# A two-layer hybrid decoder trunk on one core: moving operands of TensorE read in two interleaved runs, whole tiles as one product of 512 columns

## The chip, the core and the metric

The kernel runs on one core of one Trainium2 chip. Its time is device time in microseconds (us), median of several runs. The core has TensorE (PE in the profile, its weight loads PEld), VectorE (DVE), ScalarE (ACT), GpSimd (POOL) and SyncE (SP), an on-chip memory of 128 partitions (SBUF) and an accumulation memory (PSUM) into which TensorE writes.

## The reference

A trunk of two layers over 512 tokens of width 1,024. Layer 0 mixes tokens by attention in three groups of 8 heads (windows 128, 512 and 2,048 at dilations 1, 4 and 16, joined by a softmax over the groups), layer 1 by a gated linear recurrence with a causal convolution of four taps. Each is followed by a gated feed-forward part (FFN) with a causal convolution of three taps. Each part stands between two RMS norms and is added to the residual stream. Cut to what matters:

```python
for layer in range(DEPTH):
    h = rms_norm(x, norm_mix_pre[layer])
    h = dilated_attention_mixer(h, ...) if layer % 2 == 0 else rglru_mixer(h, ...)
    x = x + rms_norm(h, norm_mix_post[layer])
    h = rms_norm(x, norm_ffn_pre[layer])
    h = conv_ffn(h, ...)      # (gelu(conv(h @ w_up)[:D_FF]) * conv(h @ w_up)[D_FF:]) @ w_down
    x = x + rms_norm(h, norm_ffn_post[layer])

def causal_dwconv(x, w, b):   # along the tokens
    out = b
    for k in range(K):
        out = out + xp[:, k:k + S] * w[k]
    return out
```

## The kernel before

**Split products.** All large products are made in three passes: each f32 operand is split into a high part in TensorE's faster f32 format (fp32r) and a low part, the rest (`split`, L211: the high part by ACT at L212, the low part by DVE at L213), and hi*hi, hi*lo and lo*hi are added up in PSUM (`mm3`, L476, its products at L478). The profile writes f32 for these operands too. The scores S, the attention outputs O of the strided heads and the transposes tr are plain f32 products.

In `mm(dst, l, r)` the second argument is the stationary operand, loaded as weights (128 columns a load), and the third is the moving operand, whose columns stream through the array. The profile names the moving one first: `ps<-hT,whi` has hT moving, `acc<-whi,ahi` has the weight moving.

**Who moves.** There are two kinds.
- Tokens move. The normed tokens lie transposed in hT (features on the partitions, 512 tokens in a row, a high and a low copy), and a tile of 128 output features is a sum over 8 blocks of features. `feat` (L687) makes one half of a tile, 256 tokens; `feat_tile` (L720) makes both halves one after the other; `feat_tiles` can also make the first halves of several tiles before the second halves, at the start of the FFNs and of the recurrent layer, where the later tokens are not ready yet; `quarters` (L1138) makes one tile in four steps between others. The strided q and k of attention and FFN columns of blocks 2 to 11 are made by `chain` (L1157) in a scheme of seven block products instead of eight, 84 products of 256 columns for two tiles, on blocks of hT and on sums of them (T, last). `rights` (L1126) picks the moving block of each step.
- Weights move. Values (`first_values` L1293, `products` L1362) have tokens stationary and 512 columns of weights moving. The output projections of attention and recurrence (`rows_proj`, L731, `product` at L756) and the FFN's second product (`down`, L947, and `rows`, L1208) have activations stationary, 128 tokens a tile, and 512 weight columns moving, and end in acc. In the gates of the recurrent layer (L1680) tokens move, 512 columns.

**Order.** The kernel is emitted by hand in the order in which each engine runs it. Weights come in by DMA from SP (`load`, L403) and are split ahead of use by `pump` (L367), called at each `tick`; the sums of weight blocks for the chains are made by DMAs that add and by DVE. Steps of the chains stand in tables (`AT`, `QUAD`).

**Around the products.** q and k of the local heads are scaled by DVE into natural token order (`qk`, L1281); those of the strided heads are put in order of token mod 4 in the same instruction (`permute`). The convolutions read PSUM shifted by one to three columns, so the tokens must stand there in a row. The residual stream X has four tiles of 128 tokens, rows of tokens in a row; it is read from x at the start, again after attention (`x_again`, L1008), and written to out by `postnorm` (L664). The host lays out the weights before the run (`_laid_out`, L107).

Of the kernel before, what the change touches and what calls it, by code (L numbers as in the profile page):

```python
# [18 lines left out]
P = 128  # L19
S = 512  # L20
D = 1024
# [82 lines left out]
    return w.reshape(n, P, 2048)  # L104


def _laid_out(name, value):  # L107

    a = np.asarray(value)
    if name == "attn_w_qkv":  # L110
        cols, out = _column_blocks(a[0], True), []
        for kind, at, *cuts in _qkv_order():
            if kind == "value":
                rows = a[0][at * 512 : at * 512 + 512].reshape(P, 4, -1)
                out.append(np.concatenate([rows[:, :, c0 : c0 + m] for c0, m in cuts[0]], 2).reshape(P, 2048))
            else:
                out.append(cols[at // 256])
        return np.stack(out)
    if name == "lru_w_in":
        return _column_blocks(a[0], False)  # L120
    if name == "ffn_w_up":
        return np.stack([_column_blocks(w, False) for w in a])
    return a


@with_exitstack
def kernel(
# [536 lines left out]
    def postnorm(t, banks, g, final):  # L664
        at = [slice(0, 512), slice(512, 1024)]
        parts = banks
        u = [gen(s="post") for _ in at]

        def gained(i):
            nc.vector.tensor_tensor(u[i], parts[i], g[:, at[i]], op=ALU.mult)  # L670

        y = rms(parts, gained)
        for i, c in enumerate(at):
            xc = X[0][:, t, c]
            nc.vector.scalar_tensor_tensor(xc, u[i], y, xc, op0=ALU.mult, op1=ALU.add)
            if final:
                (nc.scalar if i == 1 else nc.sync).dma_start(out[0, t * P : (t + 1) * P, c], xc)

    def norms(t, banks, post_g, pre_g, hT, keep=False):
        state["hold"] = t >= 2  # L680
# [3 lines left out]
        if t == 3:  # L684
            state["hold"] = False

    def feat(W, hT, dst, n0, n1):  # L687
        for k in range(KD):
            mm3(
                dst[:, n0:n1],  # L690
                [w[k // 4][:, k % 4, :] for w in W],
                [h[:, k, n0:n1] for h in hT],
                k == 0,
                k == KD - 1,
            )

    def feat_tiles(n, hT, sink, halves=0):

        if halves:
            ids = [chunk() for _ in range(n)]  # L700
            W = {}
            banks = []
            for hf in range(2):
                for j in range(halves):
                    if not hf:
                        banks.append(psum())
                    if not hf:
                        W[j] = take(ids[j // 2], j % 2)
                    feat(W[j], hT, banks[j], hf * 256, hf * 256 + 256)
                    if hf:  # L710
                        done()
                        sink(j, banks[j])
                    tick()
            return ids
        for c in range(n):
            i = chunk()
            for m in range(2):
                feat_tile(i, m, hT, lambda ps: sink(2 * c + m, ps))

    def feat_tile(i, m, hT, sink):  # L720
# [27 lines left out]
    def rows_run(nchunks, A, prep, seq, order, post, pre, eng):  # L748
# [198 lines left out]
    def down(act, post, pre):  # L947
# [21 lines left out]
        def run(acc):  # L969
# [4 lines left out]
            for half, tiles, k in todo:  # L974
# [8 lines left out]
                for t in tiles:  # L983
                    if half and t not in second:
                        second[t] = psum("acc")
                    mm3(
                        second[t] if half else acc[t],
                        [a[:, t * P : (t + 1) * P] for a in A[k]],
                        [w[at % 2][:, 0, :] for w in W],
                        (half, k) == (1, 0),  # L990
                        k == (n - 1 if half else REST[-1]),
                    )
                    if (half, k) == (1, n - 1):
                        side(norms(t, [acc[t], second[t]], post_g, pre_g, hT))
# [128 lines left out]

    LEFT = {5: ("s1", 1), 1: ("w11", 0), 3: ("s4", 1), 2: ("w12", 0), 6: ("s2", 1), 7: ("s3", 1), 4: ("a22", 1)}

    def rights(hT, T):  # L1126

        def block(kr, n):
            return lambda h, k: hT[h][:, 4 * kr + k, n * 256 : n * 256 + 256]
# [8 lines left out]
    def quarters(i, m, hT, finish):  # L1138
        ps = []

        def quarter(n):
            W = take(i, m)
            if not n:
                ps.append(psum())
            c = slice(n % 2 * 256, n % 2 * 256 + 256)
            for k in range(4 * (n // 2), 4 * (n // 2) + 4):
                mm(ps[0][:, c], W[0][k // 4][:, k % 4, :], hT[0][:, k, c], start=n == k == 0, stop=False, skip_group_check=True)
                mm(ps[0][:, c], W[0][k // 4][:, k % 4, :], hT[1][:, k, c], start=False, stop=False, skip_group_check=True)
                mm(ps[0][:, c], W[1][k // 4][:, k % 4, :], hT[0][:, k, c], start=False, stop=k == KD - 1, skip_group_check=True)
# [44 lines left out]
    def seven(hT, T, begin, last, prep):  # L1194
# [13 lines left out]
        def rows(k, pair):  # L1208
            W, A = take(i0, ("rows", k)), take(i0, ("act", k))
            for t in pair:  # L1210
                if t not in acc:
                    acc[t] = psum("acc")
                mm3(acc[t], [a[0][:, t * P : (t + 1) * P] for a in A], [w[0] for w in W], not k, False)
            if pair[-1] == 3:
                done(2)

# [25 lines left out]
    def attention(hT, post, pre):  # L1242
# [38 lines left out]
        def qk(ps, scale, permute):  # L1281

            o = gen(s="qk")
            dst = o.rearrange("p (r u) -> p r u", r=4) if permute else o
            src = ps.rearrange("p (u r) -> p r u", r=4) if permute else ps
            row = roots[:, 512:D].rearrange("p (r u) -> p r u", r=4) if permute else roots[:, 0:512]
            if scale is not None:
                nc.vector.scalar_tensor_tensor(dst, src, scale, row, op0=ALU.mult, op1=ALU.mult)
            else:
# [3 lines left out]
        def first_values(vs):  # L1293
# [4 lines left out]
            def product(t, u, which=range(6)):  # L1298
                W = take(ids[u // 2], u % 2)
                steps = [(k, a, b) for a, b in PASSES for k in (2 * u, 2 * u + 1)]  # L1300
                for n in which:
# [1 line left out]
                    mm(  # L1303
                        banks[t],
                        hT[a][:, k, t * P : (t + 1) * P],
                        W[b][k % 2][:, 0, :],
                        start=u == n == 0,
                        stop=u == 3 and n == 5,
                    )
# [52 lines left out]
        def products(bank, t, u, W):  # L1362
            for k in (2 * u, 2 * u + 1):
                for a, b in PASSES:
                    mm(  # L1365
                        bank,
                        hT[a][:, k, t * P : (t + 1) * P],
                        W[b][k % 2][:, 0, :],
                        start=(k, a, b) == (0, 0, 0),
                        stop=(k, a, b) == (KD - 1, 1, 0),  # L1370
                    )
# [46 lines left out]
        def outputs(out, scale):  # L1418

            def top(ps):  # L1420
                out[0] = qk(ps, scale, True)

            def bottom(ps):
                out[1] = qk(ps, -1.0 if scale is None else -scale, True)

            return top, bottom

# [5 lines left out]
                vs.append(o)  # L1433

        def qk_sink(q, k):
            def f(b, ps):
                (q if b < 2 else k).append(qk(ps, SCALE if b < 2 else None, False))

            return f

# [161 lines left out]
        for hp in range(4):  # L1602
# [6 lines left out]
                side(first_sums(hT, T), 2)  # L1609
            sink = qk_sink(q, k)  # L1610
            if hp < 3:
                feat_tiles(2, hT, sink)
                for hh in range(2):
                    side(local(2 * hp + hh, hh, q, k, v), 1 + hh)
        feat_tiles(1, hT, sink)
        i = chunk()
        feat_tile(i, 0, hT, lambda ps: sink(2, ps))

        def last_local(ps, v=v):
            sink(3, ps)  # L1620
            for hh in range(2):
                side(local(6 + hh, hh, q, k, v), 0.5 + 0.5 * hh)

        fill = quarters(i, 1, hT, last_local)
# [35 lines left out]
    def lru(hT, post, pre):  # L1660
# [19 lines left out]
        def gates(n):  # L1680
            W = take(chunk(), 0)
            sg = {}
            for m in range(2):
                for gx in range(2):
                    ps = psum("gate")
                    for k in range(2):
                        mm3(ps, [w[gx][:, k, m * P : (m + 1) * P] for w in W], xs[2 * n + k], k == 0, k == 1)
# [3 lines left out]
                    nc.scalar.activation(o, ps, AF.Sigmoid, bias=cl[:, b0 : b0 + 1])  # L1691
                    sg[gx, m] = o
                if m:
                    done()
# [164 lines left out]
```

## Time and profile before

| what | value |
|---|---|
| median of 3 runs | 1393.08 us (1392.95 to 1393.39) |
| the profiled execution | 1393.96 us, its span 1392.2 us |
| granted clock of TensorE, mean | 0.998 |
| busy: ACT | 812.8 us of the span |
| busy: POOL | 236.3 us of the span |
| DMA | 214.63 MB, mean 154 GB/s |

The page gives the busy time of each engine over the span, the span in slices, the DMA queues, the chain of work that ended last, and groups of instructions with their count, busy time and mean length. The mean length of one product holds the time in which it overlaps the next one, so a run of products is shorter than the sum of their lengths. Views of the trace give the same by window, by tile or in order of time.

### The profile page before, as it was taken

To read this page: it belongs to the slowest core of one execution; us is meant where nothing else is said; L and a number is where in the kernel's file an instruction comes from. 1 tells how busy PE (TensorE), PEld (TensorE's weight loads), DVE (VectorE), ACT (ScalarE), POOL (GpSimd) and SP (SyncE) were. 2 spreads that over 40 slices of the span, in tenths; PEclk is the share of its full clock that TensorE was granted. 3 is DMA by queue.
4 is the path that set the end of the run, shared out by engine and by line. 5 is a ranking of instruction groups with operands and counts; after the bars stand their busy time and mean duration, and the time that the engine had idled before them with its cause. 6 is when DMAs were issued, how large, how long until landed. Compare 5 with 4: busy or idle time off the path is not lost.

```text
span 1392.2 us, 25651 instructions
## 1 busy us (share of the span) xinstructions
PE 1376.8 (99%) x9749; PEld 1278.5 (92%) x9749; DVE 1102.5 (79%) x2173; ACT 812.8 (58%) x1690; POOL 236.3 (17%) x392
## 2 busy tenths in 40 slices
PE   9999999999999999999999999999999999999997
PEld 7989999999998899999999888989899999999886
DVE  6576887888776899988888759768899888888853
ACT  7343565454545566666666545489576666666541
POOL 0341341222220112222120001000102222221000
PEclk9999999999999999999999999999999999999999
DMA  7553453746473556777765442421446767775511
GB/s 227 181 146 122 122 184 109 222 125 205 141 227 130 215 161 151 182 177 173 176 166 138 171 144 80 156 99 61 152 173 153 172 161 168 182 172 155 178 50 61
DMA packets 70644, 214.63 MB, mean 154 GB/s; under 512 B 10816, under 2 KB 14360, under 8 KB 58744
## 3 DMA queue, kind: packets, MB, share of 16 engines
q1 hardware_dynamic: 42552, 153.34, 32.4%
q0 software_dynamic: 27120, 58.60, 20.9%
q8 instruction: 76, 1.25, 0.4%
q10 hardware_dynamic: 848, 1.05, 0.2%
q14 instruction: 48, 0.39, 0.1%
HBM read 193.99 MB, written 18.96 MB: 153 GB/s over the span
## 4 chain that ended last, share of the span: by engine, by line
PE 76%; DVE 13%; ACT 6%; issue 3%; DMA 2%; POOL 0%; DVEq 0%; SPq 0%; ACTq 0%; POOLq 0%
PE ps L1170 32%; PE acc L478 23%; PE ps L478 8%; PE v L1365 7%; DVE wlo L213 4%; DVE u L878 2%; ACT whi L212 2%; PE v L1303 1%; DVE xb L1670 1%; PE S L1511 1%; DMA raw<-in_attn_w_qkv_dram 1%; ACT sig L1691 1%; PE O L1577 1%; PE S L1459 1%; DVE T L213 1%
## 5 line engine op out<-in xcount | busy, mean ns | idle before, releaser
L213 DVE TENSOR_TENSOR wlo<-raw,whi 128x512 fp32r<-128x512 f32 x628 | 417.5, 685 | 97.4 <-ACT whi L212 96.8
L212 ACT ACTIVATE whi<-raw 128x512 fp32r<-128x512 f32 x628 | 374.1, 626 | 154.5 <-PE acc L478 47.3
L478 PE MATMUL ps<-hT,whi 128*128 128x256 f32 x1440 | 248.9, 277 | 0.0
L1170 PE MATMUL ps<-T,whi 128*128 128x256 f32 x1344 | 239.1, 277 | 0.0
L1170 PE MATMUL ps<-hT,whi 128*128 128x256 f32 x1344 | 236.9, 276 | 0.0
L478 PEld LDWEIGHTS ps<-hT,whi 128*128 128x128 f32 x1440 | 218.0, 188 | 0.9 <-ACT whi L212 0.2
L1170 PEld LDWEIGHTS ps<-T,whi 128*128 128x128 f32 x1344 | 206.6, 188 | 3.6
L1170 PEld LDWEIGHTS ps<-hT,whi 128*128 128x128 f32 x1344 | 203.0, 188 | 0.6
L478 PE MATMUL ps<-hT,wlo 128*128 128x256 f32 x720 | 199.0, 276 | 0.4 <-DVE wlo L213 0.4
L1170 PE MATMUL ps<-T,wlo 128*128 128x256 f32 x672 | 185.8, 277 | 0.0
L1170 PE MATMUL ps<-hT,wlo 128*128 128x256 f32 x672 | 185.1, 275 | 0.0
L249 POOL DMA_DIRECT2D raw<-in_ffn_w_up_dram x120 | 104.3, 957 | 402.1 <-DVE wlo L213 369.1
L478 PEld LDWEIGHTS ps<-hT,wlo 128*128 128x128 f32 x720 | 135.4, 188 | 0.6 <-DVE wlo L213 0.6
L478 PE MATMUL acc<-whi,ahi 128*128 128x512 f32 x336 | 131.4, 391 | 0.9 <-DVE u L878 0.9
L478 PE MATMUL acc<-whi,alo 128*128 128x512 f32 x336 | 131.0, 390 | 0.2
L478 PE MATMUL acc<-wlo,ahi 128*128 128x512 f32 x336 | 130.8, 389 | 0.0
L1170 PEld LDWEIGHTS ps<-T,wlo 128*128 128x128 f32 x672 | 126.3, 188 | 0.0
L1170 PEld LDWEIGHTS ps<-hT,wlo 128*128 128x128 f32 x672 | 126.2, 188 | 0.0
L1179 ACT ACTIVATE part<-ps 128x256 f32<-128x256 f32 x168 | 63.7, 379 | 91.0 <-PE ps L1170 89.0
L1365 PE MATMUL v<-whi,hT 128*128 128x512 f32 x320 | 107.0, 397 | 0.0
L878 DVE SCALAR_TENSOR_TENSOR u<-ps,cols,u 128x511 f32<-128x511 f32 x112 | 83.6, 746 | 2.0
L1170 PE MATMUL ps<-last,whi 128*128 128x256 f32 x448 | 80.2, 278 | 2.2 <-DVE ps L1188 2.2
(227 smaller groups left out, 2439.7 us busy)
## 6 DMA issues: line engine op xcount, KB each, us to landing
raw<-in_ffn_w_up_dram SPq DMA_DIRECT2D x48, 1024.0 KB
raw<-in_attn_w_qkv_dram SPq DMA_DIRECT2D x34, 1024.0 KB
raw<-in_ffn_w_up_dram POOLq DMA_DIRECT2D x120, 256.0 KB, 5.3
raw<-in_ffn_w_down_dram SPq DMA_DIRECT2D x14, 1024.0 KB
dw<-in_ffn_w_down_dram SPq DMA_DIRECT2D x40, 256.0 KB
raw<-in_lru_w_in_dram SPq DMA_DIRECT2D x8, 1024.0 KB
turned<-T POOLq DMA_DIRECT2D x26, 256.0 KB, 2.6
ft<-turned POOLq DMA_DIRECT2D x104, 64.0 KB, 5.0
```

The costliest lines, as they stand in the source:

```text
L212: nc.scalar.activation(hi, raw, AF.Copy)
L213: nc.vector.tensor_tensor(lo, raw, hi.bitcast(F32), op=ALU.subtract)
L249: nc.gpsimd.dma_start(blocks(i)[to], plan[i][3][0][0][:, 4 * b : 4 * b + 4, :], accum_op=ALU.add)
L478: mm(dst, l[a], r[b], start=start and n == 0, stop=stop and n == 2)
L878: nc.vector.scalar_tensor_tensor(u[:, d:], ps[:, : S - d], wc, u[:, d:], op0=ALU.mult, op1=ALU.add)
L1170: mm(dst, W[wa][0][:, k, :], right[n](ha, k), start=n in (1, 5) and k == q == 0, stop=k == 3 and q == 2, skip_group_check=True,)
L1179: later(1, lambda: nc.scalar.activation(to, dst, AF.Copy))
L1303: mm(banks[t], hT[a][:, k, t * P : (t + 1) * P], W[b][k % 2][:, 0, :], start=u == n == 0, stop=u == 3 and n == 5,)
L1365: mm(bank, hT[a][:, k, t * P : (t + 1) * P], W[b][k % 2][:, 0, :], start=(k, a, b) == (0, 0, 0), stop=(k, a, b) == (KD - 1, 1, 0),)
L1459: mm(Sp[a // 2][:, o + lo : o + 256], q[hh][:, a * P : (a + 1) * P], k[hh][:, k0 : (a + 1) * P], start=True, stop=True)
L1511: mm(ps[:, c], q[hh][:, c], k[hh][:, c], start=True, stop=True)
L1577: mm(po[:, c], vtile(v, r, 2 * gi + hh), pts[gi][:, r], start=gi == 0, stop=gi == 1)
```

## The change

The moving operand of most split products is read in another order. `two` turns a row of m columns, taken as two runs of m/2, into the order 0, m/2, 1, m/2 + 1 and so on; `blocked` does this in each 256 of 512 columns. So that the results come out where they are wanted, the data is laid out for it:

- Weights that move (values, both output projections, the FFN's second product) are laid out by the host with the even columns of a block ahead of the odd ones (`_two_runs`), so that the interleaved order gives the natural one.
- From the end of attention on, a tile of tokens holds the even or the odd tokens of 256 (`of_tile`): x is read again and out is written so, and the activations that are stationary are taken with a step of two. In hT each block of 256 then holds 128 even and 128 odd tokens, and the interleaved order gives natural order for the convolutions.
- In attention itself hT keeps the natural order. The local q and k are read interleaved over 512 columns and put back by DVE (`permute=2`); attention's own chains and its tile in quarters stay as they were (`in_a_row`). The gates move interleaved tokens, and the sigmoid puts them back.
- Tiles computed whole are made by products of 512 columns instead of two halves of 256. Tiles taken in halves or quarters, and the chains, keep 256.

```diff
+def _two_runs(w):
+    return w.reshape(*w.shape[:-1], -1, 256, 2).swapaxes(-1, -2).reshape(w.shape)
...
+                rows = np.concatenate([rows[:, :, c0 : c0 + m] for c0, m in cuts[0]], 2)
+                out.append(_two_runs(rows).reshape(P, 2048))
...
+    if name in ("attn_w_o", "lru_w_out", "ffn_w_down"):
+        return _two_runs(a)
...
+    def two(ap):
+        return ap.rearrange("p (a b) -> p b a", a=2)
+
+    def of_tile(t):
+        return slice(t // 2 * 256 + t % 2, t // 2 * 256 + 256, 2)
...
-                (nc.scalar if i == 1 else nc.sync).dma_start(out[0, t * P : (t + 1) * P, c], xc)
+                (nc.scalar if i == 1 else nc.sync).dma_start(out[0, of_tile(t), c], xc)
...
-    def feat(W, hT, dst, n0, n1):
+    def feat(W, hT, dst, cols):
         for k in range(KD):
...
+            mm3(dst, [w[k // 4][:, k % 4, :] for w in W], [cols(h[:, k]) for h in hT], k == 0, k == KD - 1)
+
+    def blocked(ap):
+        return ap.rearrange("p (c a b) -> p c b a", c=2, a=2)
...
-                    feat(W[j], hT, banks[j], hf * 256, hf * 256 + 256)
+                    c = slice(hf * 256, hf * 256 + 256)
+                    feat(W[j], hT, banks[j][:, c], lambda h: two(h[:, c]))
...
-        W = take(i, m)
-        for n in (0, 256):
-            feat(W, hT, ps, n, n + 256)
+        feat(take(i, m), hT, ps, cols)
...
-                [a[:, t * P : (t + 1) * P] for a in A[k]],
-                [v[i][:, 0, cols] for v in w],
+                [a[:, of_tile(t)] for a in A[k]],
+                [two(v[i][:, 0, cols]) for v in w],
...
-            nc.sync.dma_start(X[0][:, t], x[0, t * P : (t + 1) * P, :])
+            nc.sync.dma_start(X[0][:, t], x[0, of_tile(t), :])
...
-    def rights(hT, T):
+    def rights(hT, T, cols=two):
...
-            return lambda h, k: T[n][h][k // 2][:, k % 2]
+            return lambda h, k: cols(T[n][h][k // 2][:, k % 2])
...
+    def in_a_row(ap):
+        return ap
...
-            dst = o.rearrange("p (r u) -> p r u", r=4) if permute else o
-            src = ps.rearrange("p (u r) -> p r u", r=4) if permute else ps
...
+            if permute:
+                dst, row = (a.rearrange("p (r u) -> p r u", r=permute) for a in (o, row))
+                src = ps.rearrange("p (u r) -> p r u", r=permute)
...
-                        W[b][k % 2][:, 0, :],
+                        two(W[b][k % 2][:, 0, :]),
...
-        right = rights(hT, T)
+        right = rights(hT, T, in_a_row)
...
-                    nc.scalar.activation(o, ps, AF.Sigmoid, bias=cl[:, b0 : b0 + 1])
+                    nc.scalar.activation(
+                        o.rearrange("p (r u) -> p r u", r=2), ps.rearrange("p (u r) -> p r u", r=2), AF.Sigmoid,
+                        bias=cl[:, b0 : b0 + 1],
+                    )
```

On TensorE the first tile of attention that is computed whole (ps78; hT2 is the normed tokens, whi53 and wlo54 the split weights of the first four blocks of features, whi55 and wlo56 those of the last four) stood like this before; v15 is the value product ahead of it, ps90 the next tile:

```order
L1303 MATMUL v15_159<-whi44_347,hT2_107 128x512
L478 MATMUL ps78_474<-hT2_107,whi53_406 128x256 x2
L478 MATMUL ps78_474<-hT2_107,wlo54_407 128x256
...
L478 MATMUL ps78_474<-hT2_107,whi55_410 128x256 x2
L478 MATMUL ps78_474<-hT2_107,wlo56_411 128x256
...
L478 MATMUL ps90_554<-hT2_107,whi57_420 128x256 x2
L478 MATMUL ps90_554<-hT2_107,wlo58_421 128x256
```

At the same place now:

```order
L1319 MATMUL v15_159<-whi44_347,hT2_107 128x512
L493 MATMUL ps78_474<-hT2_107,whi53_406 128x512 x2
L493 MATMUL ps78_474<-hT2_107,wlo54_407 128x512
...
L493 MATMUL ps78_474<-hT2_107,whi55_410 128x512 x2
L493 MATMUL ps78_474<-hT2_107,wlo56_411 128x512
...
L493 MATMUL ps90_530<-hT2_107,whi57_420 128x512 x2
L493 MATMUL ps90_530<-hT2_107,wlo58_421 128x512
```

Before, the rows of ps78 came twice, once for each 256 tokens, 48 products; now they come once, 24 products of 512 columns.

On TensorE at the start of the first FFN, the last tile taken in halves (ps1195) and the first one computed whole (ps1217) stood like this before:

```order
L478 MATMUL ps1195_6321<-hT1040_5664,whi1124_6013 128x256 x2
L478 MATMUL ps1195_6321<-hT1040_5664,wlo1125_6014 128x256
L478 MATMUL ps1217_6512<-hT1040_5664,whi1186_6303 128x256 x2
L478 MATMUL ps1217_6512<-hT1040_5664,wlo1187_6304 128x256
...
L478 MATMUL ps1217_6512<-hT1040_5664,whi1188_6307 128x256 x2
L478 MATMUL ps1217_6512<-hT1040_5664,wlo1189_6308 128x256
```

And now:

```order
L493 MATMUL ps1195_5961<-hT1040_5304,whi1124_5653 128x256 x2
L493 MATMUL ps1195_5961<-hT1040_5304,wlo1125_5654 128x256
L493 MATMUL ps1217_6152<-hT1040_5304,whi1186_5943 128x512 x2
L493 MATMUL ps1217_6152<-hT1040_5304,wlo1187_5944 128x512
...
L493 MATMUL ps1217_6152<-hT1040_5304,whi1188_5947 128x512 x2
L493 MATMUL ps1217_6152<-hT1040_5304,wlo1189_5948 128x512
```

The tile in halves keeps its shape and its place; the whole tile has half as many products, each twice as long. On DVE, ACT, POOL and SP every row stands where it stood.

More of the change, by code (lines that the diff above doesn't have):

```diff
@@ L685, in norms, with feat_tiles @@
             state["hold"] = False
-    def feat(W, hT, dst, n0, n1):
+    def feat(W, hT, dst, cols):
         for k in range(KD):
[L689 to L697, printed above, removed]
+            mm3(dst, [w[k // 4][:, k % 4, :] for w in W], [cols(h[:, k]) for h in hT], k == 0, k == KD - 1)
+    def blocked(ap):
+        return ap.rearrange("p (c a b) -> p c b a", c=2, a=2)
+    def feat_tiles(n, hT, sink, halves=0, cols=blocked):
         if halves:
@@ L717, in feat_tiles, with feat_tile @@
             for m in range(2):
-                feat_tile(i, m, hT, lambda ps: sink(2 * c + m, ps))
-    def feat_tile(i, m, hT, sink):
+                feat_tile(i, m, hT, lambda ps: sink(2 * c + m, ps), cols)
+    def feat_tile(i, m, hT, sink, cols=blocked):
         ps = psum()
-        W = take(i, m)
-        for n in (0, 256):
-            feat(W, hT, ps, n, n + 256)
+        feat(take(i, m), hT, ps, cols)
         done()
@@ L987, in run @@
                         second[t] if half else acc[t],
-                        [a[:, t * P : (t + 1) * P] for a in A[k]],
-                        [w[at % 2][:, 0, :] for w in W],
+                        [a[:, of_tile(t)] for a in A[k]],
+                        [two(w[at % 2][:, 0, :]) for w in W],
                         (half, k) == (1, 0),
@@ L1136, in rights, with quarters @@
         }
-    def quarters(i, m, hT, finish):
+    def in_a_row(ap):
+        return ap
+    def quarters(i, m, hT, finish, cols=two):
         ps = []
@@ L1146, in quarter @@
             for k in range(4 * (n // 2), 4 * (n // 2) + 4):
-                mm(ps[0][:, c], W[0][k // 4][:, k % 4, :], hT[0][:, k, c], start=n == k == 0, stop=False, skip_group_check=True)
-                mm(ps[0][:, c], W[0][k // 4][:, k % 4, :], hT[1][:, k, c], start=False, stop=False, skip_group_check=True)
-                mm(ps[0][:, c], W[1][k // 4][:, k % 4, :], hT[0][:, k, c], start=False, stop=k == KD - 1, skip_group_check=True)
+                mm(ps[0][:, c], W[0][k // 4][:, k % 4, :], cols(hT[0][:, k, c]), start=n == k == 0, stop=False, skip_group_check=True)
+                mm(ps[0][:, c], W[0][k // 4][:, k % 4, :], cols(hT[1][:, k, c]), start=False, stop=False, skip_group_check=True)
+                mm(ps[0][:, c], W[1][k // 4][:, k % 4, :], cols(hT[0][:, k, c]), start=False, stop=k == KD - 1, skip_group_check=True)
             if n % 2:
@@ L1212, in rows @@
                     acc[t] = psum("acc")
-                mm3(acc[t], [a[0][:, t * P : (t + 1) * P] for a in A], [w[0] for w in W], not k, False)
+                mm3(acc[t], [a[0][:, of_tile(t)] for a in A], [two(w[0]) for w in W], not k, False)
             if pair[-1] == 3:
@@ L1283, in qk @@
             o = gen(s="qk")
-            dst = o.rearrange("p (r u) -> p r u", r=4) if permute else o
-            src = ps.rearrange("p (u r) -> p r u", r=4) if permute else ps
-            row = roots[:, 512:D].rearrange("p (r u) -> p r u", r=4) if permute else roots[:, 0:512]
+            row = roots[:, 512:D] if permute == 4 else roots[:, 0:512]
+            dst, src = o, ps
+            if permute:
+                dst, row = (a.rearrange("p (r u) -> p r u", r=permute) for a in (o, row))
+                src = ps.rearrange("p (u r) -> p r u", r=permute)
             if scale is not None:
@@ L1367, in products @@
                         hT[a][:, k, t * P : (t + 1) * P],
-                        W[b][k % 2][:, 0, :],
+                        two(W[b][k % 2][:, 0, :]),
                         start=(k, a, b) == (0, 0, 0),
@@ L1420, in top @@
             def top(ps):
-                out[0] = qk(ps, scale, True)
+                out[0] = qk(ps, scale, 4)
             def bottom(ps):
-                out[1] = qk(ps, -1.0 if scale is None else -scale, True)
+                out[1] = qk(ps, -1.0 if scale is None else -scale, 4)
             return top, bottom
@@ L1435, in qk_sink, with f @@
         def qk_sink(q, k):
-            def f(b, ps):
-                (q if b < 2 else k).append(qk(ps, SCALE if b < 2 else None, False))
+            def f(b, ps, permute=2):
+                (q if b < 2 else k).append(qk(ps, SCALE if b < 2 else None, permute))
             return f
@@ L1611, in attention @@
             if hp < 3:
-                feat_tiles(2, hT, sink)
+                feat_tiles(2, hT, sink, 0, two)
                 for hh in range(2):
                     side(local(2 * hp + hh, hh, q, k, v), 1 + hh)
-        feat_tiles(1, hT, sink)
+        feat_tiles(1, hT, sink, 0, two)
         i = chunk()
-        feat_tile(i, 0, hT, lambda ps: sink(2, ps))
+        feat_tile(i, 0, hT, lambda ps: sink(2, ps), two)
         def last_local(ps, v=v):
-            sink(3, ps)
+            sink(3, ps, 0)
             for hh in range(2):
                 side(local(6 + hh, hh, q, k, v), 0.5 + 0.5 * hh)
-        fill = quarters(i, 1, hT, last_local)
+        fill = quarters(i, 1, hT, last_local, in_a_row)
         root_rows()
@@ L1686, in gates @@
                     for k in range(2):
-                        mm3(ps, [w[gx][:, k, m * P : (m + 1) * P] for w in W], xs[2 * n + k], k == 0, k == 1)
+                        mm3(ps, [w[gx][:, k, m * P : (m + 1) * P] for w in W], [two(a) for a in xs[2 * n + k]], k == 0, k == 1)
                     j = 2 * n + m
```

3 lines of the change are left out of this document (1 added, 2 removed).

## The prediction

> **What bounds the kernel now.** I read the page first: which engine is full, and at what clock.
>
> ```profile
> span 1392.2 us, 25651 instructions
> ...
> PE 1376.8 (99%) x9749; PEld 1278.5 (92%) x9749; DVE 1102.5 (79%) x2173; ACT 812.8 (58%) x1690; POOL 236.3 (17%) x392
> ...
> PEclk9999999999999999999999999999999999999999
> ```
>
> TensorE is full in every part of the span, at the full clock. Next come the waits of TensorE (who was waited for: us in total, times, longest), of which these are the first three.
>
> ```profile
> PE ps L1170 <- DVE ps L1188: 2.2, 5, 0.7
> PE warm L1778 <- DVE one L1823: 1.5, 1, 1.5
> PE gate L478 <- DVE xb L1670: 1.1, 1, 1.1
> ```
>
> The largest wait sums to 2.2 us. So the time is the number of products times their spacing; nobody else sets it. A busy mean of one product also holds its pipeline, which overlaps the next, so spacing is read from long runs in the chain in order of time (start, length, what, count).
>
> ```profile
> 33.05 27.23 PE ps L478 x240
> ...
> 60.27 1.52 PE S L1459 x8
> ...
> 220.90 8.26 PE v L1365 x36
> ...
> 449.43 3.57 PE O L1577 x32
> 453.00 27.22 PE acc L478 x120
> ...
> 563.87 9.56 PE ps L1170 x84
> 573.43 2.75 PE acc L478 x12
> ```
>
> Products of 256 columns come every 27.23/240 = 113.5 ns and 9.56/84 = 113.8 ns; products of 512 every 27.22/120 = 226.8, 8.26/36 = 229.4 and 2.75/12 = 229.2 ns. Two of 256 cost as much as one of 512: now the cost goes by the column, and nothing is paid per product.
>
> Is that the array's own rate? The trace has another kind of product to compare: the plain f32 ones of the scores, which it records as two passes each, 64 rows for the 32 products of S at L1459 (the rows below say f32 for both kinds; S, O and tr are the plain ones here).
>
> ```profile
> L478 PE MATMUL ps<-hT,whi 128*128 128x256 f32 x1440 | 248.9, 277 | 0.0
> L478 PE MATMUL acc<-whi,ahi 128*128 128x512 f32 x336 | 131.4, 391 | 0.9 <-DVE u L878 0.9
> L1459 PE MATMUL S<-qk,qk 128*128 128x256 f32 x48 | 11.7, 380 | 0.0
> L1459 PE MATMUL S<-qk,qk 128*128 128x128 f32 x16 | 3.1, 273 | 0.0
> ```
>
> An f32 pass pays 380 - 273 = 107 ns for 128 more columns, 0.84 ns a column. A split product pays 391 - 277 = 114 ns for 256 more, 0.445 ns a column. If the f32 pass takes two array steps per column, a step is 0.418 ns, and the split product loses 6% on every column. The run of eight score passes agrees: two of 128 columns and six of 256 are 14 times 256 steps, and 1.52 us/14 = 108.6 ns, where a split product of 256 takes 113.5. Both kinds read the moving operand in a row; the f32 pass has twice the time per column to fetch it and shows no loss. I read this as a fetch of the moving operand that falls a little short at one column per step. That is an inference: no run here shows the fetch by itself. The Trainium skill (TensorE: Matmul & The Clock Gate, Back-to-back issue gap) gives N/2.4 + 2.5 ns at full clock, 215.8 ns for 512 columns; the score passes fit it, the split products here, at 226.8 to 229.4 ns, do not.
>
> **The change part by part.** The order of instructions on DVE, ACT, POOL and SP is the same row for row, so only TensorE's products, the access patterns and the shapes can move time.
>
> *How many products are read in the new order.* The tile rows (PE busy and count, over the whole span) and the groups give the counts.
>
> ```profile
> 0.00:1392.20 1392.20, 817.60 (x7008) 811.32 (x7008) 256.43 (x376) 149.19 (x280) 1.00 0.54 154
> 0.00:1392.20 1392.20, 358.94 (x1536) 284.49 (x1536) 21.92 (x32) 21.27 (x64) 1.00 0.54 154
> L1365 PE MATMUL v<-whi,hT 128*128 128x512 f32 x320 | 107.0, 397 | 0.0
> L1303 PE MATMUL v<-whi,hT 128*128 128x512 f32 x64 | 19.0, 404 | 1.0 <-ACT whi L212 1.0
> L478 PE MATMUL gate<-xhi,whi 128*128 128x512 f32 x32 | 12.7, 395 | 1.8 <-DVE xb L1670 1.1 <-ACT sig L1691 0.6
> ```
>
> Of 7,008 products of 256 (ps, first row), attention keeps 16 chains of 84 and one tile of 48 in a row: 1,392. Tiles computed whole, 15 in attention, 11 in the recurrent layer and 3 in each FFN, 32 times 48 = 1,536, become 768 products of 512. The rest, 4,080 (40 chains of 84, 13 tiles taken in halves and 2 in quarters at 48 each), stay at 256, interleaved. Products of 512: 1,536 into acc (second row), v 320 + 160 and 64 + 32 (each lo pass for two hi passes), gates 3 x 32: 2,208, all interleaved. At 113.6 and 228 ns these two kinds are 796 + 503 = 1,299 us of the 1,376.8 busy.
>
> *What a product costs when read so.* No row shows it. If the loss goes, a product of 512 takes two units of the score run, 217 ns. A product of 256 has a weight load for every 256 steps, and its nearest rows are the score run at 108.6 and the 32 passes of O, 3.57/32 = 111.6 ns, each with its load. I take the middle, 110.1, and keep both ends.
>
> - 2,208 of 512: 228 (between 226.8 and 229.4) to 217, 11 ns: 24.3 us.
> - 768 merged: two of 113.5 to 217, 10 ns: 7.7 us. Merging alone gains nothing; it pays only if a cost per product comes into view.
> - 4,080 of 256: 113.7 to 110.1, 3.6 ns: 14.7 us (8.6 at 111.6, 20.8 at 108.6).
> - 1,392 left in a row, and the f32 passes: nothing.
>
> The sum is 46.7 us. Part of it is given back where DVE is nearly full (PE, PEld, DVE, ACT, POOL busy).
>
> ```profile
> 520.00:540.00 20.00, 20.00 (x179) 20.00 (x178) 19.12 (x32) 12.48 (x24) 4.67 (x7) 1.00 0.68 143
> 1050.00:1070.00 20.00, 20.00 (x179) 20.00 (x178) 19.12 (x32) 13.23 (x25) 5.16 (x6) 1.00 0.70 146
> ...
> sum 120.00, PE 119.60 PEld 118.22 DVE 112.45 ACT 81.28 POOL 22.50; mean PE 19.93 PEld 19.70 DVE 18.74 ACT 13.55 POOL 3.75
> 576.18:588.49 12.31, 12.31 (x98) 11.81 (x98) 10.66 (x18) 7.56 (x15) 2.61 (x3) 1.00 0.71 172
> ```
>
> At the start of each FFN (500 to 560 and 1030 to 1090) DVE works 112.45 of 120 us; TensorE would want those in some 115.5, so of 4.5 us gained there I give back most, 4 us with the odd wait elsewhere. In the chains (last row: one cycle of 84 + 12 products) TensorE would go from 12.31 to 84 x 110.1 + 12 x 217 = 11.85 us; DVE's 10.66 still fits, and the DMA share rises from 0.71 to 0.74.
>
> *Edits that I cost at nothing.* The local q and k are now put back in order by DVE while it scales them, as the strided ones already are:
>
> ```profile
> L1288 DVE SCALAR_TENSOR_TENSOR qk<-ps,roots x32: 680/688/697, 49.2 to 417.9; 128x512 f32<-128x512 f32 x32
> L1583 DVE TENSOR_TENSOR o<-O,o 128x512 f32<-128x512 f32 x8 | 8.6, 1079 | 2.6 <-PE O L1577 2.3
> L1691 ACT ACTIVATE sig<-gate,cols 128x512 f32<-128x512 f32 x16 | 9.7, 708 | 0.0
> ```
>
> The 32 rows (min/median/max) hold both orders and all take 680 to 697 ns: zero. The 16 sigmoids read PSUM in steps and write in a row; I take zero too, since the q and k case is nearest. The far end is L1583, which steps on both sides: 1079 - 708 = 371 ns, 16 of them 6 us on ACT, beside TensorE's work. The tokens as stationary operand of rows and down are now every other element:
>
> ```profile
> L608 PEld LDWEIGHTS tr<-ident,x_sb 128*128 128x128 f32 x24 | 3.9, 207 | 0.7 <-issue 0.5
> L588 PEld LDWEIGHTS tr<-ident,xs 128*128 128x128 f32 x72 | 8.2, 140 | 0.4
> 12.03 0.65 PEld L608 LDWEIGHTS tr<-ident,x_sb 128*128 128x128 f32 x4
> ```
>
> L608 loads every fourth element: 207 ns against 140 in a row (L588), and four of them in 0.65 us come (0.65 - 0.207)/3 = 148 ns apart. Every second element should lie below that, and a product of 512 covers 217. Nothing, unless such a load passed 217. The rows of x and out go to other tokens in the same DMAs of the same size: nothing.
>
> So 1393.96 (the profiled execution) - 46.7 + 4 = 1351.3, and the median of the runs, 1393.08, lies 0.9 lower: **1350.4 us**, say 1350.
>
> **The rivals.**
> - *One fetch serves two runs, half the loss stays.* If the loss is a pause at each new piece of a run, and the pauses of both runs fall together, half of 46.7 goes: 1393.96 - 23.3 + 1 = 1371.7, median 1371. Nothing in the trace prefers whole to half; that both runs cross their pieces side by side speaks for it.
> - *The change doesn't touch the loss.* If each piece costs its pause whichever run it is in, the same number of pieces is read and the time stays at 1393, within 3 us. For it: the loss is the same for hT, T, weights and last as moving operand, at 113.5 to 113.8, so where the data lies does not matter. Against it: the f32 passes read the same way without loss.
> - *Every change of run is paid, slower.* If the reader keeps only one piece open, each column of the interleaved order opens a piece anew. Price: the stepped load, 207 - 140 = 67 ns over 128 elements, 0.52 ns a column. On 4,080 x 256 + 2,976 x 512 = 2.57 million columns that is 1,344 us: about 2,738 us. It decides from 46.7 us/2.57 million = 0.018 ns a column on, so a small part of that price is enough. The Trainium skill (Advanced Engine Details and Errata, SBUF Cachelines) states such a rule: lines of 16 bytes, full speed if the next access hits the same line, a penalty for a different line each time; by it this order is the bad one. The trace agrees as far as a load with every element in a line of its own is dearer; no run here shows a moving operand so read. Against this rival: in the new order each piece is used up over four turns, not once as in L608.
>
> **How the numbers follow.** All of the loss goes: 0.56. Half of it: 0.14. Untouched: 0.11. Every change of run paid: 0.17. Left for what I don't see: 0.02. The forecast is the first case, 1350. Its bounds: 111.6 for every 256 and 226.8 for 512 now give 2,208 x 9.8 + 7.7 + 8.6 = 37.9 us, less 4: 1359. With 229.4 for 512 now, 108.6 for 256, and nothing given back it is 27.4 + 7.7 + 20.8 = 55.9: 1337. The slope alone, 0.418 ns a column with no cost per product (214 and 107 ns), is the far end: 2,208 x 15.4 + 768 x 13 + 4,080 x 6.7 = 71 us, 1322. I set the low end between these two, 1330, and the high end past the untouched case, 1397; that leaves out the 0.17 and 0.02. A difference of 0.2% (2.8 us) is about what a measurement of this kernel can tell. The untouched case is 0.09 within that and 0.02 a little faster, by the merged products. Faster: 0.56 + 0.14 + 0.02 = 0.72; same: 0.09; slower: 0.17 and the unseen 0.02, 0.19.
>
> **What would show it.** Right: runs of 84 chain products take about 9.25 us for 9.56, 12 of acc 2.60 for 2.75, whole tiles of attention 217 ns for each product of 512, while attention's own chains stay at 27.47 us for 240; waits of TensorE for DVE appear around the two FFN starts. Half: 9.4 and 2.67. Untouched: all runs as before. Wrong: spacings above 114 and 230, or acc products held at the spacing of the weight loads.

## The result and the profile after

| | median us | runs |
|---|---|---|
| before, same chip | 1393.01 | 1392.53 to 1393.39 (4) |
| after | 1367.26 | 1366.6 to 1369.2 (4) |

The ratio is 0.9818, 95% interval 0.9801 to 0.9835: 25.8 us faster, where 43 were forecast. The profiled execution of the changed kernel took 1369.20 us, 24.8 less than that of before. One of the ten executions of merging alone, below, took 2817.14 us and is left out; the trace of that run is of this execution, so no spacing is read from it. The page of the changed kernel begins so:

```profile
span 1367.4 us, 24126 instructions
...
PE 1338.2 (98%) x8981; PEld 1255.3 (92%) x8981; DVE 1103.7 (81%) x2173; ACT 807.7 (59%) x1690; POOL 236.4 (17%) x392
```

768 products and as many weight loads are gone. The work of DVE and ACT is within 1% of what it was, in a shorter span. The chain in order of time (start, length, what, count) shows the spacings; L1184 is the step of a chain, L1170 before.

```profile
33.88 25.90 PE ps L493 x120
...
354.27 7.77 PE v L1381 x36
370.10 27.46 PE ps L1184 x240
...
557.13 9.38 PE ps L1184 x84
566.51 2.60 PE acc L493 x12
```

Products of 512 come every 25.90/120 = 215.8, 7.77/36 = 215.8 and 2.60/12 = 216.7 ns, with tokens or with weights moving. The FFN's chains come every 9.38/84 = 111.7 ns. Attention's chains, whose order was left alone, keep 27.46/240 = 114.4. The groups (mean ns behind the busy time) show the rest of what was forecast:

```profile
L493 PE MATMUL acc<-whi,ahi 128*128 128x512 f32 x336 | 128.0, 381 | 1.8 <-DVE u L889 1.8
L1475 PE MATMUL S<-qk,qk 128*128 128x256 f32 x48 | 11.7, 380 | 0.0
L493 PEld LDWEIGHTS acc<-whi,ahi 128*128 128x128 f32 x336 | 65.9, 196 | 9.2 <-issue 2.5 <-ACT ahi L220 0.3
L1304 DVE SCALAR_TENSOR_TENSOR qk<-ps,roots 128x512 f32<-128x512 f32 x32 | 22.0, 689 | 17.6 <-DMA roots<-yrow 11.3 <-PE ps L1184 3.8 <-PE ps L493 2.2
L1707 ACT ACTIVATE sig<-gate,cols 128x512 f32<-128x512 f32 x16 | 9.7, 702 | 0.0
```

A split product of 512 now equals an f32 pass of 256, 381 against 380 ns. The load of every second token takes 196 ns for 188 and hides under 216. q, k and the sigmoids cost what they cost. What did not stay as it was are the waits of TensorE (us in total, times, longest):

```profile
PE ps L1184 <- DVE ps L1202: 6.5, 5, 2.0
PE gate L493 <- DVE xb L1686: 2.9, 1, 2.9
PE tr L603 <- ACT B L593: 2.0, 2, 1.1
PE O L1593 <- DMA toe<-rowv: 1.8, 1, 1.8
PE acc L493 <- DVE u L889: 1.8, 2, 0.9
PE acc L493 <- DVE alo L221: 1.6, 2, 1.4
```

These six sum to 16.6 us, the whole view to 21.0; the whole view of before summed to 7.9. Windows at the start of the first FFN and one cycle of its chains (the columns are those of the windows before):

```profile
512.00:532.00 20.00, 19.86 (x147) 18.81 (x146) 19.83 (x33) 10.96 (x22) 5.44 (x7) 1.00 0.58 126
532.00:550.00 18.00, 16.84 (x140) 16.41 (x138) 15.89 (x26) 13.65 (x27) 3.96 (x5) 1.00 0.78 169
...
569.11:581.09 11.98, 11.98 (x99) 11.74 (x98) 10.55 (x18) 7.43 (x15) 2.61 (x3) 1.00 0.74 178
```

DVE is full for 20 us (19.83), and in the 18 us behind it TensorE stands 1.2 us, at the end, for an addition of DVE. That DVE's load alone makes this wait is not shown: in these 18 us DVE is busy for 15.89, and 3 us before the end of the wait it stood 0.78 us itself, for a split of ACT. In the chains (last row) DVE fits, as forecast.

The longest wait has a cost of its own. Behind it the granted clock (third number from the end of a window's row) was half for 3.41 us:

```profile
903.96 0.45 PE L493 MATMUL gate<-xhi,whi 128*128 128x512 f32 x1 [2.86 <-DVE xb L1686]
...
904.90:908.31 3.41, 3.15 (x8) 2.06 (x7) 1.56 (x3) 3.41 (x8) 0.00 (x0) 0.50 0.12 18
```

In this stretch gate products that waited for nothing came up to 427 ns apart instead of 216, so up to 1.7 us went (half of 3.41). Before, the longest wait was 1.5 us, and the clock was full from the first microseconds to the last.

By stage, from the first product of one to the first of the next, the span fell so: attention with its projection 484.9 to 477.6 us; the starts of the two FFNs, up to the first chain product that reads `last`, 57.7 to 57.6 and 57.7 to 57.9; the rest of the FFNs 312.8 to 304.6 and 311.1 to 302.9; the recurrent layer 158.8 to 157.2. The FFN starts gained nothing, the recurrent layer 1.6 us.

### The profile page after: what moved, and what is told of

Read it like the earlier page. It is cut to its first block, busy times and chain, and to the rows that moved or that the text cites. A ratio compares the mean times of both kernels' runs of the same rounds, so it can differ in the third digit from the quotient of the medians.

```text
span 1367.4 us, 24126 instructions
## 1 busy us (share of the span) xinstructions
PE 1338.2 (98%) x8981; PEld 1255.3 (92%) x8981; DVE 1103.7 (81%) x2173; ACT 807.7 (59%) x1690; POOL 236.4 (17%) x392
## 4 chain that ended last, share of the span: by engine, by line
PE 62%; issue 19%; DVE 11%; DMA 5%; ACT 3%; POOL 0%; DVEq 0%; POOLq 0%; ACTq 0%; SPq 0%
PE ps L1184 31%; PE acc L493 16%; PE ps L493 6%; PE v L1381 6%; DVE wlo L221 4%; DMA raw<-in_attn_w_qkv_dram 2%; DVE u L889 1%; DMA raw<-in_ffn_w_up_dram 1%; PE v L1319 1%; PE S L1527 1%; ACT whi L220 1%; DMA ft<-turned 1%; PE S L1475 1%; PE O L493 1%; DVE ps L1197 0%
## 5 line engine op out<-in xcount | busy, mean ns | idle before, releaser
L1184 PE MATMUL ps<-T,whi 128*128 128x256 f32 x1344 | 235.6, 276 | 0.3
L1184 PE MATMUL ps<-hT,whi 128*128 128x256 f32 x1344 | 235.0, 276 | 0.0
L493 PE MATMUL ps<-hT,whi 128*128 128x512 f32 (+1 forms) x928 | 223.8, 334 | 0.2 <-ACT whi L220 0.2
L1184 PEld LDWEIGHTS ps<-T,whi 128*128 128x128 f32 x1344 | 207.4, 191 | 2.9 <-ACT part L1193 0.7
L1184 PEld LDWEIGHTS ps<-hT,whi 128*128 128x128 f32 x1344 | 204.3, 191 | 0.7 <-ACT part L1193 0.2
L1184 PE MATMUL ps<-T,wlo 128*128 128x256 f32 x672 | 185.3, 276 | 0.0
L1184 PE MATMUL ps<-hT,wlo 128*128 128x256 f32 x672 | 185.1, 275 | 0.0
L493 PEld LDWEIGHTS ps<-hT,whi 128*128 128x128 f32 x928 | 159.7, 190 | 13.9 <-ACT whi L220 0.4
L493 PE MATMUL ps<-hT,wlo 128*128 128x512 f32 (+1 forms) x464 | 154.3, 333 | 0.4 <-DVE wlo L221 0.4
L493 PE MATMUL acc<-whi,ahi 128*128 128x512 f32 x336 | 128.0, 381 | 1.8 <-DVE u L889 1.8
L1184 PEld LDWEIGHTS ps<-T,wlo 128*128 128x128 f32 x672 | 128.2, 191 | 0.0
L1184 PEld LDWEIGHTS ps<-hT,wlo 128*128 128x128 f32 x672 | 128.2, 191 | 0.0
L493 PE MATMUL acc<-wlo,ahi 128*128 128x512 f32 x336 | 127.3, 379 | 0.0
L1381 PE MATMUL v<-whi,hT 128*128 128x512 f32 x320 | 102.7, 384 | 0.0
L493 PEld LDWEIGHTS ps<-hT,wlo 128*128 128x128 f32 x464 | 88.3, 190 | 7.5 <-DVE wlo L221 0.6
L1184 PE MATMUL ps<-last,whi 128*128 128x256 f32 x448 | 79.5, 278 | 6.5 <-DVE ps L1202 6.5
```

Source lines behind the costliest of these rows:

```text
L493: mm(dst, l[a], r[b], start=start and n == 0, stop=stop and n == 2)
L1184: mm(dst, W[wa][0][:, k, :], right[n](ha, k), start=n in (1, 5) and k == q == 0, stop=k == 3 and q == 2, skip_group_check=True,)
L1381: mm(bank, hT[a][:, k, t * P : (t + 1) * P], two(W[b][k % 2][:, 0, :]), start=(k, a, b) == (0, 0, 0), stop=(k, a, b) == (KD - 1, 1, 0),)
```

## The experiments

**The orders by themselves.** A program of its own, 24 runs of 40 products with nothing beside them. The moving operand m holds split-format data (fp32r); each run reads it in one order, for instance:

```diff
+    def two(n):
+        return m[:, :n].rearrange("p (a b) -> p b a", a=2)
+
+    def near(n, c):
+        return m[:, :n].rearrange("p (b a c) -> p b c a", a=2, c=c)
...
+    run("inrow512", rows(512))
+    run("two512", two(512))
...
+    run("two256narrow", two(256), 64)
...
+    run("pairs512", m[:, :512].rearrange("p (a b c) -> p b a c", a=2, c=2))
...
+    run("near4x512", near(512, 4))
```

> A program of its own, which computes nothing of the reference: 24 runs of 40 split-format products with nothing else at work, each run with one reading order of the moving operand, width of the stationary operand, or step of the stationary operand. Theory (the fetch of a moving row falls short by about 6% per column, interleaving two runs removes that, and a product of 256 is then held by its weight load at 111.7 ns): in a row 227 ns for 512 and 113.4 for 256; two runs, 128 or 256 elements apart, 216 for 512; two runs at 256 columns 111.7 with 128 stationary columns and 109 with 64, while in a row 256 stays at 113.4 with 64 too; products of 128 columns at 111.7 in either order. Rival (half of the loss stays where the runs are 128 apart): blocked 512 near 222, and 256 at 111.7 also with 64 stationary columns. Rival (a cost per product of some 5 ns): 256 interleaved stays at 111.7 with 64 stationary columns and 128 columns come at 59 or less. For the smaller questions: a stationary operand with a step of two costs nothing under 512 columns (227 and 216); by the rule of full speed within a line of 16 bytes, pairs and fours taken in turn would be faster than single elements, and a step of four the slowest of all.

Its TensorE in order of time (start, length, the run's name, columns, 40 products each). The spacing is the next run's start less this one's, over 40.

```profile
17.57 9.41 PE L46 MATMUL inrow<-both 128*128 128x512 f32 x40
26.82 8.79 PE L46 MATMUL two<-both 128*128 128x512 f32 x40
35.45 8.80 PE L46 MATMUL blocked<-both 128*128 128x512 f32 x40
44.08 4.76 PE L46 MATMUL inrow<-both 128*128 128x256 f32 x40
48.68 4.62 PE L46 MATMUL two<-both 128*128 128x256 f32 x40
53.14 4.96 PE L46 MATMUL inrow256narrow<-both 128*64 128x256 f32 x40
57.94 4.53 PE L46 MATMUL two256narrow<-both 128*64 128x256 f32 x40
62.30 4.58 PE L46 MATMUL inrow<-both 128*128 128x128 f32 x40
66.72 4.63 PE L46 MATMUL two<-both 128*128 128x128 f32 x40
...
89.21 13.26 PE L46 MATMUL pairs<-both 128*128 128x512 f32 x40
102.29 10.10 PE L46 MATMUL fours<-both 128*128 128x512 f32 x40
112.23 11.19 PE L46 MATMUL fourruns<-both 128*128 128x512 f32 x40
...
141.37 18.31 PE L46 MATMUL step2x<-both 128*128 128x512 f32 x40
159.50 9.51 PE L46 MATMUL step4x<-both 128*128 128x256 f32 x40
...
168.83 8.82 PE L46 MATMUL near4x<-both 128*128 128x512 f32 x40
177.49 8.80 PE L46 MATMUL near8x<-both 128*128 128x512 f32 x40
```

512 in a row: (26.82 - 17.57)/40 = 231 ns. Two runs, 256 or 128 apart: 216, so the distance does not matter, down to four elements (near4x, 216.5). 256 in a row 115, in two runs 111.5, and with half as many stationary columns (128*64) 109: then the load no longer holds it. 128 columns take 110.5 in a row, far above half of 115: loads do not come faster than that. So the theory's reason for 111.7 holds, and both rivals for it fall. In a row with 64 stationary columns the product came slower, 120 ns, which was not expected. Wrong was the guess about pairs and fours: taken in turn they cost 13.08/40 = 327 and 9.94/40 = 248 ns, and reading only every second element 18.13/40 = 453. A step of four took 9.33/40 = 233 ns for 256 columns, the slowest by the column, as expected. A weight load with a step of two cost nothing beside interleaved products (216) and 4 ns beside products in a row (235 for 231).

**Where the loss in a row comes from.** A second program of its own, with the weights at other places relative to the moving data, fewer stationary columns, 2-byte data and plain f32:

```diff
+    for off in (4, 8, 12, 20, 36, 40):
+        run(f"rowat{off}x", row, w_at(off))
...
+    for cols in (32, 64, 96):
+        run(f"rowcols{cols}x", row, w_at(40), cols)
+    run("halfwordrow", bm[:, :512], bw)
...
+    run("plainrow", raw[:, 0:256], raw[:, D : 2 * D])
```

> A second program of its own: runs of 40 products alone on the chip, for the cause of the loss in a row. Theory (the fetch of a 4-byte moving operand falls short at one column per step): 512 columns of 2-byte data in a row take 216 ns, plain f32 in a row 216 for a pass of 256, neither better when interleaved; split products in a row stay at 226 to 231 wherever the weights lie and however many columns are loaded. Rival (the moving read and the weight load clash in the memory): the time in a row changes by 5 ns or more with the place of the weights, reaching 216 at some, and shrinks towards 216 with 96, 64 and 32 stationary columns.

The same view of this program; a plain f32 product is two passes, so 80 rows a run.

```profile
19.54 9.49 PE L49 MATMUL rowat4x<-both 128*128 128x512 f32 x40
28.87 9.23 PE L49 MATMUL rowat8x<-both 128*128 128x512 f32 x40
37.94 9.23 PE L49 MATMUL rowat12x<-both 128*128 128x512 f32 x40
...
74.74 8.80 PE L49 MATMUL twoat4x<-both 128*128 128x512 f32 x40
...
100.64 9.25 PE L49 MATMUL rowcols32x<-both 128*32 128x512 f32 x40
109.73 9.41 PE L49 MATMUL rowcols64x<-both 128*64 128x512 f32 x40
...
128.05 8.81 PE L49 MATMUL halfwordrow<-half 128*128 128x512 bf16 x40
136.69 19.54 PE L49 MATMUL halfwordtwo<-half 128*128 128x512 bf16 x40
156.07 9.20 PE L49 MATMUL halfwordstep<-half 128*128 128x512 bf16 x40
165.10 17.43 PE L49 MATMUL plainrow<-raw 128*128 128x256 f32 x80
182.37 22.02 PE L49 MATMUL plaintwo<-raw 128*128 128x256 f32 x80
204.23 18.29 PE L49 MATMUL plainstep<-raw 128*128 128x256 f32 x80
222.16 9.60 PE L49 MATMUL last<-both 128*128 128x512 f32 x40
```

In a row, split products never fall below 227 ns (rowat8x, 9.07/40), with 128 stationary columns or 32: the loss is in the moving read. The place of the weights adds up to 6 ns to it (rowat4x, 233), and the interleaved order does not feel it (twoat4x, 216). So the rival has a part: the place does matter, by more than the 226 to 231 expected, but no place and no number of columns comes near 216. 2-byte data in a row takes 216 and plain f32 216: no loss, as the theory had it. But interleaved they are much worse, 19.38/40 = 484 and 21.86/80 = 273 ns. "Neither better" was right and far too mild.

**Merging alone.** Before, with whole tiles as one product, in a row.

```diff
-        for n in (0, 256):
-            feat(W, hT, ps, n, n + 256)
+        feat(W, hT, ps, 0, 512)
```

> Before, with the whole tiles as one product of 512 columns read in a row; nothing interleaved. Theory: 768 products at 227 replace 1,536 at 113.5, so no change, 1393 within 2 us. Rival (the gain comes from fewer products and weight loads): 8 us faster or more, 1385.

Ratio to before 1.0012 (1.0002 to 1.0021), 1394.8 us against 1393.3. Merging by itself gains nothing.

**The order alone.** The changed kernel, whole tiles again as two products of 256, interleaved.

```diff
+    def half_of(v, n):
+        return v[:, n] if len(v.shape) == 4 else v[:, n * 128 : n * 128 + 128]
...
-        feat(take(i, m), hT, ps, cols)
+        W = take(i, m)
+        for n in range(2):
+            feat(W, hT, ps[:, n * 256 : n * 256 + 256], lambda h: half_of(cols(h), n))
```

> The changed kernel, with the whole tiles as two products of 256 columns again, each read interleaved. Theory: 1,536 products at 111.7 for 768 at 216, 768 x 7.4 = 5.7 us slower than the changed kernel, some of it hidden where TensorE waits: 1371 to 1373. Rival (merging carries the gain): 1380 or more.

1368.83 us, ratio 0.9816 (0.9796 to 0.9836): not to be told from the changed kernel (0.9818, 0.9801 to 0.9835), and below the 1371 to 1373 expected. Its run of products has the price, though (120 products of 512 in 25.90 us above):

```profile
32.28 26.80 PE ps L493 x240
```

240 of 256 take 26.80 us, 0.9 more; over all whole tiles, 6.4 times as many products, 5.8 us. The profiled execution was 4.0 us slower than that of the changed kernel, the median 1.6; with runs from 1365.9 to 1373.24, how much of the price reaches the time can't be told. The rival falls: the order carries the gain.

**Attention's chains interleaved too.** The runs are four elements apart here, and DVE takes the order back to token mod 4 by two instructions of 256 instead of one of 512.

```diff
+            if permute == 4:
+                for a in range(2):
+                    dst, rw = (t.rearrange("p (r b a) -> p a r b", r=4, a=2)[:, a] for t in (o, row))
+                    src = ps.rearrange("p (b r a) -> p a r b", r=4, a=2)[:, a]
...
-        right = rights(hT, T, in_a_row)
+        right = rights(hT, T, lambda ap: ap.rearrange("p (b a c) -> p b c a", a=2, c=4))
```

> The changed kernel, with attention's own chains interleaved as well, in another order: two runs four elements apart (0, 4, 1, 5, 2, 6, 3, 7, 8, 12 and so on), which DVE puts in order of token mod 4 by two instructions of 256 instead of one of 512. Theory: 1,344 products from 113.8 to 111.6 free 3 us on TensorE; 32 times some 160 ns more on DVE lie beside it, but attention already waits for DVE and for DMA, so between nothing and 3 us faster than the changed kernel: 1364 to 1367. Rival (the distance of the runs matters in the kernel, where other engines write to the same memory): the chains stay at 113.8 or rise, 1367 or more.

With it ran the changed kernel once more, on the same chip:

> The changed kernel once more, beside the next three on the same chip: 1366 to 1369.

The changed kernel took 1367.42 us, this one 1366.95 (ratios to before 0.9811 and 0.9813, 0.9795 to 0.9827 and 0.9799 to 0.9828): no difference. The chains are faster. Of the changed kernel and of this one, the chain and the longest wait within attention (150 to 440 us):

```profile
229.41 27.46 PE ps L1184 x240
...
PE ps L1184 <- DVE ps L1202: 3.4, 3, 1.7
```

```profile
229.78 26.80 PE ps L1184 x240
...
PE ps L1184 <- DVE ps L1202: 5.2, 3, 3.3
```

240 products fell from 27.46 to 26.80 us, so the order works there as well, and the wait for DVE rose from 3.4 to 5.2 us. That this swallows the gain is not shown by it alone: DVE has more to do here (64 instructions of some 440 ns for 32 of 686, 3 us in all), and attention is unsteady, 477.6 us in one trace of the changed kernel and 472.7 in this second one, while their other stages agree to 0.4 us.

**Less work for DVE, after and before.** The convolutions of both kernels lose taps: the FFN's the last one, the recurrent layer's the last two. The output is then another one; TensorE's work is the same.

```diff
-                for d, wc in ((1, near[:, 48 + j : 49 + j]), (2, far[:, j : j + 1])):
+                for d, wc in ((1, near[:, 48 + j : 49 + j]),):
...
-            for d in (1, 2, 3):
+            for d in (1,):
```

> The changed kernel without the last tap of the FFN's convolution and the last two of the recurrent layer's, which leaves out 96 and 16 instructions of 749 ns on DVE and none on TensorE. Theory (some 18 us of TensorE's gain are given back in waits, mostly for DVE): the waits at the FFN starts, the gates and the last products shrink, 5 to 9 us faster than the changed kernel, 1358 to 1362. Rival (the gain is short because products take longer somewhere, not because of waits): 0 to 2 us faster, as in the kernel before.

> The kernel before, with the same instructions left out: 112 x 749 ns = 84 us of DVE. Theory: TensorE was the bound and waited little for DVE, 1 to 3 us faster than before, 1390 to 1392. Rival (DVE set part of the time before as well): 5 us or more.

The changed kernel fell to 1353.74 us, 13.7 less; the kernel before to 1386.95, 6.7 less (ratios to before 0.9707, 0.9687 to 0.9728, and 0.9954, 0.9937 to 0.9970). Both fell by more than expected, and the kernel before as its rival had it: DVE set some of the time before as well. The difference of 7.0 us, uncertain by some 4 us by the intervals, is what the same DVE work costs more once TensorE is faster. The first waits of TensorE, of the changed kernel with fewer taps and of before with fewer taps:

```profile
PE ps L1184 <- DVE ps L1202: 2.6, 2, 2.0
PE tr L603 <- ACT B L593: 1.9, 2, 1.0
```

```profile
...
PE ps L1170 <- DVE ps L1188: 0.9, 2, 0.6
```

The waits at the gates and for the last u of the FFN, 2.9 and 1.8 us above, are no longer among them. From the first gate to the output projection of the recurrent layer the traces show 77.6 to 72.5 us for the changed kernel and 78.6 to 76.3 for before; the FFN starts shrink by 0.3 to 0.6 us and by nothing. The rival (longer products) falls for these 7.0 us.

## Why the prediction was right, and where not

**The mechanism.** The first case came true for the spacings: all of the loss goes. Products of 512 at 216 ns, 217 forecast. The inference behind it, that the moving read in a row is short for split data and not for plain f32, is shown by the second program; why such a read is short is not.

**The sum.** Products of 512: 2,208 x (228 - 216) = 26.5 us, forecast 24.3. Merged tiles: 768 x (2 x 113.5 - 215.8) = 8.6, forecast 7.7. Products of 256: 4,080 x (113.8 - 111.7) = 8.6, forecast 14.7. There the middle was taken between a row with its loads at 111.6 and one at 108.6; the loads hold these products, so the 111.6 of O was the right row and the middle was not. Together 43.7 us, forecast 46.7.

**The step that was mis-sized** is what is given back: 4 us forecast, 43.7 - 24.8 = 18.9 in the profiled execution. TensorE's idle time accounts for 13.8 of it: its busy time fell by 38.7 us, from 1376.83 to 1338.16, the span by 24.8, so that idle time rose from 15.4 to 29.2. The other 5 us are waits as well, which the busy time hides. From the start of each product to the start of the next, all that lies above the usual spacing of its kind in its trace sums to 17.8 us before and 37.5 now, 19.7 more: within 1 us all that was given back, so that no slower product is needed to explain it. The end of a product counts as busy for some 0.16 us of each wait behind it (3.24 us between two starts at the gates show as a wait of 2.86, where 216 ns are usual), and products at half the clock count as busy throughout.

The step counted on the FFN starts, and there it was right: what was gained went, in both. It was the "odd wait elsewhere" that it had at next to nothing. Of the 19.7 us, 8.9 lie in attention with its projection, 5.6 in the recurrent layer and 5.2 in the FFNs. I looked for DVE's share in two stretches of 60 us, on average; elsewhere TensorE comes earlier to a norm, a gate or a sum that DVE must finish, and stands there. The reading under it, that nobody but TensorE sets the time, was off as well: fewer taps on DVE made the kernel before 6.7 us faster. The fewer taps put some 7 us of what was given back on DVE in the FFNs and the recurrent layer. How attention's part splits between ACT, DMA and DVE was not tried, and there two traces of the changed kernel differ by 4.9 us.

**The range.** 1367 lies outside the 1337 to 1359 that were worked out for the first case. It is inside 1330 to 1397 only because the high end was set past the untouched case; that was luck, as no term of the sum foresaw these waits.

**The rivals.** "Half of the loss stays" said 1371, and 1367 lies nearer to it than to 1350. By the time alone it would have won; the spacings rule it out, none of 512 lies at 222. "Untouched" is ruled out by the same rows. "Every change of run is paid" is wrong for split data and right for the others: 2-byte data went from 216 to 484 ns in this very order, 268/512 = 0.52 ns a column, the price that was put on it. The Trainium skill (Advanced Engine Details and Errata, SBUF Cachelines) has the rule behind it, and the runs agree for 2-byte and plain f32 data. For split data they do not: pairs, with two elements of a line at a time, take 327 ns, and single elements in turn are the fastest order found. There the measurement decides against the rule. Weighing it at 0.17 was fair; nothing in the trace of before could tell.

**The edits at nothing** were nothing: q and k 689 ns, sigmoids 702, stepped loads 196 under 216. That merging alone gains nothing was right, and that it pays 5.8 us beside the order was right for TensorE (7.7 forecast) and not to be told from the spread of the runs in the time.

## What to carry to other kernels

If an engine is busy 99% of the time, compare its rate with another kind of work of its own in the same trace: 108.6 against 113.5 ns for the same array steps pointed at a loss that no wait shows. The gain from a faster engine is the sum over its products less what its neighbours, who were just fast enough, then hold up; where DVE was at 94% of a stretch all of the gain was given back, and most of what was lost lay at hand-overs in stages where DVE was at 80%: count them one by one. And a reading order belongs to a data type: measure it for that type alone before changing a layout.

## What the runs showed that I had not expected

- For split (fp32r) moving operands, alternating between two runs single element by single element takes 216 ns for 512, as 2-byte and plain f32 data do in a row, whatever the distance from 4 to 256 elements; in a row 227 to 233, in pairs 327, every second element 453. The cause of this ranking stays open.
- The same order takes 2-byte data from 216 to 484 ns and a plain f32 pass of 256 from 216 to 273, while a step of two costs these two little: 9.03/40 = 226 and 17.93/80 = 224 ns.
- A weight load of 128 columns bounds products of up to 256 columns at 110.5 to 111.5 ns; with 64 columns 109. The Trainium skill (TensorE: Matmul & The Clock Gate, LDWEIGHTS) gives P/1.2, 107 ns for 128 columns; the runs lie 4 to 5 ns above.
- In a row, the place of the weights relative to the moving data is worth up to 6 ns of 227; interleaved, none.
- The changed kernel's runs spread over 2.6 and 4.6 us in two sets of four, those of before over 0.9 to 2.4 in sets of 4 to 13. Between two traces of the changed kernel the difference lies in attention, where the waits are longest in sum; that waits make a time less steady fits this, and is not shown.
- Short waits cost clock: behind waits of 2 to 3.5 us the granted clock was half for 3.41 us at least once in every trace of the changed kernel and its variants, and in neither trace of the kernel before, whole and with fewer taps (waits of at most 1.5 us), first and last microseconds aside. Not every such wait did it: behind one of 2.01 us the clock stayed full.
